# Three shared PSUM banks for projections and transposes in the two attention stages of a hybrid decoder step

## The chip, the cores and the metric

The kernel runs on one NeuronCore of a Trainium2 chip. The metric is the device time of one launch in microseconds (us), taken as the median of the runs shown. All stretches below are in us from the start of the profiled span.

## The reference, cut to what matters

One step of a decoder with two layers runs over 1024 prompt tokens and 8 sample tokens, 1032 columns together. Each layer is a norm, one input projection for all heads, two kinds of heads side by side, an output projection and an MLP:

```python
# layer 0: differential attention (4 heads) and HGRN2 (4 heads)
qa, ka, va, qb, fb, ib, gb = _split(h @ w_in, SPLIT_EVEN)
p = probs(q1, k1) - lam * probs(q2, k2)            # softmax over all earlier keys
return jnp.einsum('bqhk,bkhe->bqhe', ...)          # attention output
# layer 1: forgetting attention (8 heads) and mLSTM (4 heads)
qc, kc, vc, fc, qd, kd, vd, id_, fd, od = _split(h @ w_in, SPLIT_ODD)
s = s + fq - fk                                    # bias from the forget gates
```

The prompt attends to itself. Each of the 8 sample tokens attends to 512 cached tokens, in four pages of 128 that a page table picks from a pool. This second part is called the decode here.

## The kernel before

All activations lie transposed, 128 features on the partitions and 1032 tokens along the columns. A projection makes one block of 128 output features from 8 chunks of the 1024 inputs. It does so for three token blocks of 344 columns, and each of these needs 24 matmuls, since float32 accuracy is had from three passes (`mm3`, L119). The 24 matmuls gather in one PSUM bank, which VectorE then empties into the tile `z` (L183, or L185 with a constant). Below, "block" means such a token block: 24 matmuls and one eviction.

An attention stage is the part of `run` in which the prompt's attention of one layer is computed. Layer 0 has it from about 157 to 517 us and layer 1 from about 1573 to 1987 us. Three strands of work are mixed in it:

- The attention itself (`diff_head`, `fox_head`): scores into the tile `S` (L517, L519, L520), row minimum on VectorE (L535, L537), exponential on ScalarE (L539), transposes of the probabilities into the tile `pm` (L557), the split of these into two parts (`Ph` on ScalarE at L545, `Pl` on VectorE at L546), and the products with the values into the tile `po` (L573). The values are transposed as well (L591, L1067).
- Projections as filler (`self.fill`): 27 blocks for the queries, keys and values of the later heads, then 24 blocks for the layer's other kind of heads. `tick` traces some of them after each score block, and `drain` traces what is left of a list.
- The decode as background (`self.back`, `diff_sample` and `fox_sample`). It begins when the sample queries, which the projections leave in `qa_s` or `qc_s`, are transposed (L659) and written to DRAM (L663). Then each of the 32 key pages is loaded (L653), multiplied on GpSimd (L675) and summed on VectorE (L676). After a softmax each of the 32 value pages is loaded, multiplied (L691) and summed (L692). Four tiles `dk` hold pages. All these loads are issued by SyncE, in order.

The order of the instructions on each engine is not written by hand. A scheduler takes the traced program and places instructions as their operands and a slot of their tile's pool come free; a tile's pool and tag say which slots it may take. In both attention stages PSUM's eight banks are given as follows: four to `S` (two tiles of two banks), one to `po`, two to the tag `m` (all transposes and small products, named `pm` and `hms`) and one to the tag `acc` (the projections).

Of the kernel before, what the change touches and what calls it, by code (L numbers as in the profile page):

```python
# [10 lines left out]
F32 = mybir.dt.float32  # L11
# [7 lines left out]
D = 1024          # model width  # L19
NP = 1024         # prompt tokens  # L20
NS = 8            # sample tokens (one per sequence)
T = NP + NS       # columns of every transposed activation
TB = 344          # token block of a projection
NTB = T // TB
KC = D // 128     # contraction chunks of a projection
NCH = NP // 128   # token chunks of 128
PAGES = 4
# [3 lines left out]
LN_MIN = 1e-19    # smallest argument that Ln is given  # L31
# [5 lines left out]
# columns of the packed per-partition parameters  # L37
# [7 lines left out]
class Tags:  # L45
    """Pools of a phase, stacked in the order in which their tiles are done with (or wanted); tags pick the pool."""
# [9 lines left out]
class Step:  # L56
    """The whole step: two trunk layers over 1032 transposed columns."""

    def __init__(self, tc, ctx, I, O):
# [20 lines left out]
        # scratch in DRAM  # L80
# [11 lines left out]
    def wsplit(self, src, kk, m=128, parts=None):  # L92
        """Loads a block of weights and splits it into two float32r parts."""
        nc = self.nc
        r = self.wr.tile([128, 8, 128], F32, name="wr")
        h, l = parts or (self.wh.tile([128, 8, 128], F32R, name="wh"), self.wl.tile([128, 8, 128], F32R, name="wl"))
        nc.sync.dma_start(r[:, :kk, :m], src)
        nc.scalar.activation(h[:, :kk, :m], r[:, :kk, :m], AF.Copy)  # L98
        nc.gpsimd.tensor_tensor(l[:, :kk, :m], r[:, :kk, :m], raw(h[:, :kk, :m]), op=ALU.subtract)  # L99
        return h, l  # L100

    def first_block(self, src):
        """wsplit of the block that the whole core waits for, in pieces."""
# [9 lines left out]
    def mm3(self, out, h, l, ah, al, ks, sl, m=128):  # L113
        """out = W^T a with float32 accuracy from three float32r passes."""
# [7 lines left out]
    def project(self, ps, src, evict, m=128, w=None):  # L122
        """One block of output features; yields after each token block."""
        h, l = w or self.wsplit(src, KC, m)
        for tb in range(NTB):
            sl = slice(tb * TB, (tb + 1) * TB)
            pt = ps.tile([128, 512], F32, name="acc", tag="acc")
# [4 lines left out]
    def project_rms(self, ps, src, evict, rms, w=None):  # L132
        """The first block of a phase: its products run while 1/rms is still being computed."""
# [9 lines left out]
    def project_to(self, pool, ps, src, dst, scale=None, keep=None, done=None):  # L143
        """A block of output features into DRAM (and its sample columns into keep)."""
# [11 lines left out]
    def tick(self, n=1.0):  # L156
        """Traces the next pieces of the filler work (projections) and of the background work (decode)."""
# [12 lines left out]
    def drain(self, k, upto=None):  # L170
        """Traces what is left of a kind of work (up to and with one generator)."""
# [4 lines left out]
    def scaled(self, dst, scale=None):  # L176
        """Eviction of a projection: times the token's 1/rms (and a constant)."""
# [11 lines left out]
    def gain(self, x, n, gcol, hi, lo):  # L189
        """x * gain of chunk n, split into two float32r parts (the last chunk by token blocks, as it is waited for)."""  # L190
# [16 lines left out]
    def rms(self, pool, ps, sq=None, t0=0, n=T):  # L207
        """rb[:, t] = 1 / sqrt(mean_d x[t, d]^2 + eps) on every partition, for n tokens from t0."""
# [25 lines left out]
    def head_norm(self, sm, po, pm, dst, gcol, gate, n, eps=None, thr=None):  # L234
        """dst = po * rsqrt(mean over partitions of po^2 + eps) * gain (* gate); po stays in PSUM."""
# [17 lines left out]
    def hgrn_gates(self, ph, ps, pr, first):  # L253
        """f = lb + (1 - lb) sigmoid(.) and silu(g) of all heads, into DRAM."""
# [32 lines left out]
        # orders the first Ln behind the last Sigmoid (one table switch)  # L287
# [4 lines left out]
    def ln_exp(self, last):  # L292
        """One table set with both Ln and Exp, loaded behind the layer's last Sigmoid."""
# [3 lines left out]
    def hgrn_unit(self, h, u, ph, ps):  # L297
        """Half of a head's tokens (four chunks), in steps.

        Decays are products of the gates f. With blocks of hh tokens, QP holds q times the product of f from the  # L300
        block's start through the token, KR holds k times the product behind the token to the block's end, and
        pe the products of whole blocks; each level joins pairs of blocks, from 1 token up to a chunk of 128."""
# [17 lines left out]
        # A^T[s, t]: the diagonal, then one level of the binary tree of decays at a time  # L320
# [29 lines left out]
        # rows of the decayed k, states after each chunk  # L350
# [23 lines left out]
        # o^T = i^T A^T + S^T (q e^b), normalised and gated  # L374
# [11 lines left out]
    def staggered(self, units, lag):  # L386
        """Traces units in turn, each some steps behind the one before."""
# [12 lines left out]
    def hgrn_sample(self, ph, ps):  # L400
        """One step of the HGRN2 states: S' = f S + k i, o = q^T S'."""
# [41 lines left out]
    def diff_consts(self, ph, ps):  # L443
        """lambda, the constants made from it, and the Toeplitz tiles of the relative bias."""
# [9 lines left out]
        # c = max(1, |lambda|): probabilities are kept as (p1 - lambda p2) / c  # L454
        nc.vector.tensor_scalar(lc[:, 1:2], lc[:, 0:1], -1.0, 1.0, op0=ALU.mult, op1=ALU.max)
        nc.vector.tensor_tensor(lc[:, 1:2], lc[:, 1:2], lc[:, 0:1], op=ALU.max)
        nc.vector.reciprocal(lc[:, 2:3], lc[:, 1:2])                                    # 1 / c
# [1104 lines left out]
```

## Time and profile before

| quantity | value |
|---|---|
| median of 3 runs | 2928.14 us (2927.41 to 2929.16) |
| span of the profiled execution | 2917.3 us |
| what lies around the span (median less span) | 10.8 us |
| TensorE busy | 2769.9 us, 95% of the span |
| VectorE, ScalarE, GpSimd busy | 1285.9, 891.8 and 871.3 us |
| mean granted clock of TensorE | 0.967 of full speed |

The profile gives no time of its own for the profiled execution besides the span, so the runs' median is set beside it. TensorE is busy nearly all the time in the two MLPs, which fill most of the span. The two attention stages are 774 us together, and it is there that TensorE idles and that its clock falls.

### The profile page before, as it was taken

Reading aid. Unit: us, or ns where it says so; the run is one execution under the profiler, and the core shown is the slowest. Engines: PE = TensorE matmul, PEld = TensorE weight load, DVE = VectorE, ACT = ScalarE, POOL = GpSimd, SP = SyncE. Lnnn points to the kernel's source line nnn. Section 1 sums busy time; section 2 is a strip of 40 time slices with the busy share of each in tenths; the row PEclk is TensorE's granted clock in tenths of the full one; section 3 lists DMA queues with packets and bytes.
Section 4 is the critical chain, followed back from the end, with each engine's and each line's share of the span. In section 5 each row is a group of like instructions: output and inputs, shape, how many; then the busy total and the mean of one; then the engine's idle time right before and its main releaser. Section 6 shows DMA issues by size and latency. Waiting matters only on the chain.

```text
span 2917.3 us, 43680 instructions
## 1 busy us (share of the span) xinstructions
PE 2769.9 (95%) x17276; PEld 2646.3 (91%) x17276; DVE 1285.9 (44%) x2433; ACT 891.8 (31%) x1546; POOL 871.3 (30%) x689
## 2 busy tenths in 40 slices
PE   8999889899999999999999989679999999999997
PEld 7988778898999999999998988577889999999997
DVE  5154866675532233322435455465463333223335
ACT  4143434114321222222323434343342222222223
POOL 2322753354222212222122254331242222221222
PEclk9999999899999999999999999887999999999998
DMA  3343686633111111111224354875331111111111
GB/s 135 117 145 98 200 219 194 167 109 99 48 51 51 48 39 45 52 51 54 74 98 126 115 169 124 164 190 136 105 98 47 37 48 51 51 48 37 48 62 66
DMA packets 167103, 278.48 MB, mean 95 GB/s; under 512 B 25159, under 2 KB 86375, under 8 KB 166899
## 3 DMA queue, kind: packets, MB, share of 16 engines
q1 hardware_dynamic: 166562, 275.42, 31.8%
q8 instruction: 136, 2.23, 0.3%
q0 software_dynamic: 336, 0.28, 0.1%
q14 instruction: 69, 0.56, 0.1%
HBM read 226.53 MB, written 49.11 MB: 94 GB/s over the span
## 4 chain that ended last, share of the span: by engine, by line
PE 79%; DMA 9%; DVE 5%; POOL 2%; issue 2%; ACT 1%; SPq 1%; DVEq 0%; POOLq 0%; ACTq 0%
PE acc L119 69%; DMA dp<-p_c 1%; PE pm L338 1%; PE po L573 1%; PE S L520 1%; PE S L517 1%; DMA kd<-out_ka 1%; PE pm L557 1%; DMA dk<-in_cache_k_c 1%; DMA dI<-irow 1%; POOL dk L691 1%; DMA dk<-in_cache_v_a 1%; POOL dk L675 1%; DMA ol<-os 1%; DMA dk<-in_cache_v_c 1%
## 5 line engine op out<-in xcount | busy, mean ns | idle before, releaser
L119 PE MATMUL acc<-xh,wh 128*128 128x344 f32 (+1 forms) x2808 | 919.2, 328 | 38.6 <-DVE z L183 28.0
L119 PE MATMUL acc<-xl,wh 128*128 128x344 f32 (+1 forms) x2808 | 909.1, 324 | 1.0 <-DVE xl L195 0.9
L99 POOL TENSOR_TENSOR wl<-wr,wh 128x512 fp32r<-128x512 f32 (+1 forms) x284 | 504.5, 1777 | 1350.0 <-ACT wh L98 1347.4
L119 PE MATMUL acc<-xh,wl 128*128 128x344 f32 (+1 forms) x2808 | 902.0, 323 | 3.8 <-POOL wl L99 3.8
L119 PEld LDWEIGHTS acc<-xh,wh 128*128 128x128 f32 (+1 forms) x2808 | 536.3, 191 | 52.2 <-DVE z L183 31.9
L119 PEld LDWEIGHTS acc<-xh,wl 128*128 128x128 f32 (+1 forms) x2808 | 534.8, 191 | 5.6 <-POOL wl L99 4.7
L119 PEld LDWEIGHTS acc<-xl,wh 128*128 128x128 f32 (+1 forms) x2808 | 536.1, 191 | 3.2 <-DVE xl L195 2.3
L98 ACT ACTIVATE wh<-wr 128x512 fp32r<-128x512 f32 (+1 forms) x284 | 228.3, 805 | 974.5 <-PE acc L119 844.2
L119 PE MATMUL acc<-ul,wh 128*128 128x344 f32 (+1 forms) x1568 | 495.6, 317 | 0.2 <-DVE ul L1178 0.2
L119 PE MATMUL acc<-uh,wl 128*128 128x344 f32 (+1 forms) x1568 | 493.9, 317 | 1.5 <-POOL wl L99 1.5
L119 PE MATMUL acc<-uh,wh 128*128 128x344 f32 (+1 forms) x1568 | 493.0, 317 | 1.6 <-ACT wh L98 1.6
L1243 DVE TENSOR_TENSOR x<-acc,x 128x344 f32<-128x344 f32 x336 | 173.5, 516 | 438.1 <-PE acc L119 438.1
L119 PEld LDWEIGHTS acc<-uh,wh 128*128 128x128 f32 x1568 | 294.0, 188 | 2.1 <-ACT wh L98 2.0
L119 PEld LDWEIGHTS acc<-uh,wl 128*128 128x128 f32 x1568 | 293.6, 188 | 2.1 <-POOL wl L99 2.1
L119 PEld LDWEIGHTS acc<-ul,wh 128*128 128x128 f32 x1568 | 294.5, 188 | 0.7 <-DVE ul L1178 0.6
L1230 DVE TENSOR_TENSOR ul<-u,uh 128x344 fp32r<-128x344 f32 x192 | 146.0, 762 | 202.2 <-ACT uh L1229 202.2
L1227 DVE SCALAR_TENSOR_TENSOR t<-acc,rb 128x344 f32<-128x344 f32 x192 | 98.6, 516 | 267.7 <-PE acc L119 265.7
L1228 ACT ACTIVATE u<-t 128x344 f32<-128x344 f32 x192 | 93.8, 490 | 323.5 <-DVE t L1227 322.5
L183 DVE TENSOR_TENSOR z<-acc,rb 128x344 f32<-128x344 f32 x138 | 69.9, 512 | 200.1 <-PE acc L119 183.5
L539 ACT ACTIVATE e<-S,st 128x128 f32<-128x128 f32 (+7 forms) x128 | 94.6, 740 | 145.7 <-DVE st L537 70.2
L691 POOL TENSOR_TENSOR dk<-dk,dp 128x512 f32<-128x512 f32 x64 | 84.3, 1334 | 104.9 <-DMA dk<-in_cache_v_c 43.2
L675 POOL TENSOR_TENSOR dk<-dk,dq 128x512 f32<-128x512 f32 x64 | 84.7, 1347 | 43.3 <-DMA dk<-in_cache_k_c 18.1
(377 smaller groups left out, 3289.8 us busy)
## 6 DMA issues: line engine op xcount, KB each, us to landing
wr<-in_w_up SPq DMA_DIRECT2D x64, 512.0 KB
wr<-in_w_down SPq DMA_DIRECT2D x128, 256.0 KB
wr<-in_w_in_e SPq DMA_DIRECT2D x27, 512.0 KB
wr<-in_w_out SPq DMA_DIRECT2D x48, 256.0 KB
wr<-in_w_in_o SPq DMA_DIRECT2D x24, 512.0 KB
x<-in_x SPq DMA_DIRECT2D x16, 516.0 KB
qd<-qS SPq DMA_DIRECT2D x32, 256.0 KB
dk<-in_cache_k_a SPq DMA_DIRECT2D x32, 256.0 KB
```

The lines of the kernel that those rows point to most:

```text
L98: nc.scalar.activation(h[:, :kk, :m], r[:, :kk, :m], AF.Copy)
L99: nc.gpsimd.tensor_tensor(l[:, :kk, :m], r[:, :kk, :m], raw(h[:, :kk, :m]), op=ALU.subtract)
L119: nc.tensor.matmul(out, lhsT=w[:, k, :m], rhs=a[:, sl], start=(n == 0), stop=(n == last))
L183: nc.vector.tensor_tensor(dst[:, sl], p, rb[:m, sl], op=ALU.mult)
L338: nc.tensor.matmul(pt[:, 64 * c:64 * c + 64].rearrange("p (n t) -> p n t", t=hh), lhsT=k[:, 128 * c:128 * c + 128], rhs=Q[:, n0:n0 + 64 // ...
L539: nc.scalar.activation(e[:, :L], S[:, :L], AF.Exp, bias=st[:, 0:1], scale=-1.0, accum_out=st[:, 1:2])
L675: nc.gpsimd.tensor_tensor(kt[:], kt[:], qb[:], op=ALU.mult)
L691: nc.gpsimd.tensor_tensor(v3, v3, pb[:, :, js], op=ALU.mult)
L1227: nc.vector.scalar_tensor_tensor(t[:], pt[:, :TB], 0.0, self.rb[:, sl], op0=ALU.max, op1=ALU.mult)
L1228: nc.scalar.activation(u[:], t[:], AF.Square)
L1230: nc.vector.tensor_tensor(L[:, sl], u[:], raw(H[:, sl]), op=ALU.subtract)
L1243: nc.vector.tensor_tensor(x[:, sl], pt[:, :TB], self.x[n][:, sl], op=ALU.add)
```

## The change

In both attention stages the projections' own pool (`acc1`, `acc4`) is gone. The pool of the transposes gets three banks under its tag `m`, and the projections take their tiles from that tag. Everywhere else `acc_tag` is `"acc"`, as it was. The tile's name stays `acc`, so that the same rows can be found by name. The layer-1 stage is changed in the same way as layer 0, with `pS4`, `pm4` and `acc4`.

```diff
     def project(self, ps, src, evict, m=128, w=None):
...
-            pt = ps.tile([128, 512], F32, name="acc", tag="acc")
+            pt = ps.tile([128, 512], F32, name="acc", tag=self.acc_tag)
             self.mm3(pt[:m, :TB], h, l, self.xh, self.xl, range(KC), sl, m)
...
         self.credit = {}
+        self.acc_tag = "acc"
...
-            pS, pm, acc = self.pool(st, "pS1", 2, True), self.pool(st, "pm1", 2, True), self.pool(st, "acc1", 1, True)
+            pS, pm = self.pool(st, "pS1", 2, True), self.pool(st, "pm1", 3, True)
+            acc, self.acc_tag = pm, "m"
             hd = self.pools(st, "hd0", "ld dp dk dq row32 sc ov pr tr pse oso dst", "Q1 K1 K2 bias st rl", "z e")
...
             self.drain("fill")
             self.drain("back")
+            self.acc_tag = "acc"
```

The scheduler makes another order of both stages. The first place is TensorE in the attention stage of layer 0, where the transpose of the sample queries stands (`pm` from `qa_s`, L659). The number behind a tile's name rises in the order in which tiles were traced. Before, it stands here, behind the last rows of the block `acc_2220`:

```order
L119 MATMUL acc_2220<-xl7_185,wh_2215 128x344
L119 MATMUL acc_2220<-xh7_184,wl_2216 128x344
L659 MATMUL pm_2537<-ident_72,qa_s_90 32x128
L591 MATMUL pm_2587<-ident_72,vt_2583 128x128 x4
L591 MATMUL pm_2594<-ident_72,vt_2583 128x128 x4
L119 MATMUL acc_2261<-xh0_122,wh_2215 128x344
```

With the change the same transpose, now `pm_2534`, stands here:

```order
L517 MATMUL S_2714<-K1_2428,Q1_2427 128x512
L520 MATMUL S_2714<-K2_2408,Q1_2427 128x512
L240 MATMUL hms_2500<-hsq_2498,ones_73 128x512
L659 MATMUL pm_2534<-ident_72,qa_s_90 32x128
L591 MATMUL pm_2584<-ident_72,vt_2580 128x128 x4
L517 MATMUL S_2807<-K1_2416,Q1_2415 128x512
```

Before, the transpose was taken ahead of blocks that were traced earlier: `acc_2261` comes behind `pm_2537`. With the change every tile of the tag `m` stands in traced order, in both stages, and six more blocks (144 matmuls of L119) stand ahead of the transpose.

The second place is TensorE in the attention stage of layer 1, at the transpose of its sample queries (`pm` from `qc_s`). Before:

```order
L119 MATMUL acc_15690<-xl7_13832,wh_15685 128x344
L119 MATMUL acc_15690<-xh7_13831,wl_15686 128x344
L659 MATMUL pm_15955<-ident_72,qc_s_93 32x128
L557 MATMUL pm_16071<-ident_72,e_15919 128x128
L557 MATMUL pm_16071<-ident_72,e_15999 128x128
```

With the change:

```order
L119 MATMUL acc_15922<-xl7_13828,wh_15917 128x344
L119 MATMUL acc_15922<-xh7_13827,wl_15918 128x344
L659 MATMUL pm_15948<-ident_72,qc_s_93 32x128
L119 MATMUL acc_15995<-xh0_13429,wh_15917 128x344
L119 MATMUL acc_15995<-xl0_13430,wh_15917 128x344
```

Here too the transpose waits for all blocks traced before it (`acc_15922` has a number just below `pm_15948`), which again are 144 more matmuls of L119 than before.

The third place is VectorE at the end of the decode of layer 1, where the last page is summed (the second `ov` row). Before:

```order
L692 TENSOR_REDUCE ov<-dk 128x4
L546 TENSOR_TENSOR Pl<-pm,Ph 128x512
L756 TENSOR_REDUCE oso<-ov 128x32
L183 TENSOR_TENSOR z<-acc,rb 128x344
L757 TENSOR_TENSOR oso<-oso,pse 128x32
L1092 RECIPROCAL st<-st 128x1
L1096 TENSOR_SCALAR e<-e,st 128x896
```

With the change:

```order
L692 TENSOR_REDUCE ov<-dk 128x4 x2
L756 TENSOR_REDUCE oso<-ov 128x32
L183 TENSOR_TENSOR z<-acc,rb 128x344
L757 TENSOR_TENSOR oso<-oso,pse 128x32
L1432 CAST triT<-triTf 128x512
L183 TENSOR_TENSOR z<-acc,rb 128x344
L546 TENSOR_TENSOR Pl<-pm,Ph 128x512 x3
```

Behind the last sum VectorE still had 8 row minima (L535) and 19 splits (L546) of the stage to do before; with the change 4 and 14 are left.

## Rows read from the trace of the kernel before

**Rows 1.** The page: span, and busy time of each engine.

```profile
span 2917.3 us, 43680 instructions
PE 2769.9 (95%) x17276; PEld 2646.3 (91%) x17276; DVE 1285.9 (44%) x2433; ACT 891.8 (31%) x1546; POOL 871.3 (30%) x689
```

**Rows 2.** Windows: stretch, its length, busy time by engine, granted clock, DMA share, GB/s.

```profile
157.00:281.00 124.00, 121.68 (x689) 104.31 (x688) 63.33 (x151) 50.27 (x98) 25.82 (x18) 1.00 0.36 115
281.00:381.00 100.00, 92.30 (x507) 77.92 (x506) 75.02 (x146) 41.49 (x78) 61.50 (x44) 0.95 0.67 192
381.00:478.00 97.00, 85.18 (x425) 71.01 (x425) 68.65 (x141) 37.21 (x70) 57.20 (x38) 0.89 0.85 215
478.00:517.00 39.00, 35.27 (x219) 30.90 (x217) 20.50 (x47) 18.55 (x34) 2.58 (x2) 1.00 0.54 181
1573.00:1690.00 117.00, 107.67 (x697) 102.30 (x696) 52.30 (x96) 47.64 (x87) 27.65 (x18) 0.99 0.39 121
1690.00:1836.00 146.00, 128.88 (x799) 118.25 (x797) 85.40 (x156) 59.63 (x113) 71.02 (x80) 0.93 0.57 148
1836.00:1946.00 110.00, 72.90 (x388) 66.43 (x388) 57.28 (x104) 33.02 (x66) 51.02 (x37) 0.77 0.79 182
1946.00:1987.00 41.00, 36.94 (x231) 32.18 (x231) 24.22 (x49) 26.47 (x52) 2.30 (x9) 0.92 0.45 149
...
506.00:517.00 11.00, 7.33 (x50) 5.87 (x48) 6.48 (x19) 4.71 (x8) 1.28 (x1) 1.00 0.62 210
```

**Rows 3.** TensorE's eviction waits in 157:285, 285:517 (two), 1570:1692, 1692:1987: total, times, longest.

```profile
PE acc L119 <- DVE z L183: 2.0, 3, 0.7
...
PE acc L119 <- DVE z L183: 7.7, 5, 3.8
...
PE acc L119 <- DVE z L185: 1.9, 2, 1.7
...
PE acc L119 <- DVE z L183: 5.2, 8, 0.7
...
PE acc L119 <- DVE z L183: 13.2, 6, 5.1
```

**Rows 4.** The chain that ended last: start, length, what.

```profile
48.83 102.42 PE acc L119 x650
...
264.88 4.07 PE acc L119 x24
...
274.29 4.00 PE acc L119 x24
...
1657.62 4.05 PE acc L119 x24
...
1685.81 4.02 PE acc L119 x24
1690.52 2.55 DMA qrow_c<-row
```

**Rows 5.** Timeline of TensorE near 300 us: the start of two score pairs.

```profile
299.25 0.50 PE L517 MATMUL S<-K,Q 128*128 128x512 f32 x1
...
300.11 0.50 PE L517 MATMUL S<-K,Q 128*128 128x512 f32 x1
```

**Rows 6.** Timeline of GpSimd at the start of layer 0's decode.

```profile
279.00 0.71 POOL L663 DMA_DIRECT2D qrow_a<-row  x1 [1.94 <-ACT row L661]
286.42 8.07 POOL L675 TENSOR_TENSOR dk<-dk,dq 128x512 f32<-128x512 f32 x6 [6.72 <-DMA dq<-qrow_a]
```

**Rows 7.** Waits in 1836:1946 of VectorE, GpSimd, SyncE; last, VectorE in 360:480.

```profile
DVE ov L692 <- POOL dk L691: 50.6, 19, 8.0
...
POOL dk L691 <- DMA dk<-in_cache_v_c: 43.2, 12, 6.2
...
SPq L1165 <- POOL dk L691: 24.0, 10, 3.3
...
DVE ov L692 <- POOL dk L691: 19.6, 12, 3.2
```

More of the change, by code (lines that the diff above doesn't have):

```diff
@@ L1388, in run @@
             self.drain("back")
+            self.acc_tag = "acc"
         with ExitStack() as st:
@@ L1400, in run @@
         with ExitStack() as st:
-            pS, pm, acc = self.pool(st, "pS4", 2, True), self.pool(st, "pm4", 2, True), self.pool(st, "acc4", 1, True)
+            pS, pm = self.pool(st, "pS4", 2, True), self.pool(st, "pm4", 3, True)
+            acc, self.acc_tag = pm, "m"
             hd = self.pools(st, "hd1", "ld dp dk dq row32 sc lg sfx ov pr lfe pse oso dst lgg", "Q1 K1 K2 Q20 Q21 st", "z e")
@@ L1419, in run @@
             self.drain("back")
+            self.acc_tag = "acc"
         with ExitStack() as st:
@@ L1432, in run @@
             self.drain("back")
+            self.acc_tag = "acc"
         with ExitStack() as st:
```

## The prediction

> **What bounds the kernel now.** I began with the page [rows 1]: TensorE is busy 2769.9 of 2917.3 us, so at most 147 us lie idle. The table of windows [rows 2] shows the two attention stages, the only places that the change touches: 774 us, with TensorE busy in 681. Read it by stretch. Each stage opens with a stretch full of TensorE work: 121.7 of 124 us and 107.7 of 117, at a granted clock of 1.00 and 0.99. Then the decode starts [rows 6], and the bound changes. While the value pages pass (381 to 478 and 1836 to 1946), TensorE is busy in 85.2 of 97 us and 72.9 of 110, the clock falls to 0.89 and 0.77, and the DMA engines are the fullest thing, at 0.85 and 0.79. There VectorE waits for GpSimd's products (19.6 us in layer 0, 50.6 in layer 1), GpSimd waits for the pages (43.2), and SyncE waits for GpSimd to free a tile (24.0) [rows 7]. This ring of load, product, sum and next load has only four page tiles; it runs at its own pace, and everything queued behind a sum on VectorE waits with it. Once the decode is over, TensorE leads again for 39 and 41 us.
>
> So a stage is a chain of three parts: work before the decode's start (A), the decode (B), and what is left behind it (tail). A transfer of PSUM matters as far as it changes A, B or the tail.
>
> **What the change removes.** With one bank a block's first matmul waits until VectorE has emptied the block before. These waits sum to 2.0 + 7.7 + 1.9 + 5.2 + 13.2 = 30.0 us in both stages [rows 3]; that is the most they can give. Where blocks follow each other with nothing between, the chain shows the price: six intervals from 1657.62 to 1685.81 are 28.19 us, 4.70 each, while an unbroken run of 650 such matmuls takes 102.42 us, 0.158 each and 3.78 for 24 [rows 4]. Each such block wastes 0.92 us. Layer 1 has eight in a row, 7.4 us in A. In layer 0 the three blocks from 264.88 to the transpose at about 278.1 take 13.3 instead of 11.3 us: 2.0.
>
> The waits inside B (7.7 + 1.9 and 13.2, less what lies in the tail) stand in stretches that the decode paces. I bound their worth by 0 and 22.8 us and take 6, three for each layer, nearer to the lower end, since in 1836 to 1946 TensorE idles 37 us in any case.
>
> **What it moves.** Projections and transposes now take slots of one tag, and the order shows that they take them in traced order. Before, the transposes went ahead: the sample queries' transpose L659 stood ahead of blocks traced earlier. Now it stands behind all of them, 144 matmuls later in each stage: six blocks of 3.78 us, 22.7. Fewer scores stand ahead of it in return: six pairs in layer 0, four in layer 1. A 512-wide pair takes 0.86 us (299.25 to 300.11) [rows 5], so at most 5.2 and 3.4; many are narrower in layer 0, so I take 4.0 and 3.4. Everything that starts the decode hangs on L659: ScalarE's copy, GpSimd's transfer at 279.00, SyncE's query loads, and the first product at 286.42 [rows 6]. On SyncE the page loads, weights and the next heads' keys are queued behind the query loads, so they move too. A grows by
>
> - layer 0: 22.7 - 4.0 - 2.0 = +16.7 us
> - layer 1: 22.7 - 3.4 - 7.4 = +11.9 us
>
> TensorE has as much less to do later. That pays only where TensorE leads. In B of layer 0 four fewer evictions stand on VectorE among the decode's sums. If TensorE led there, 15 us would come back; if the decode leads, nothing. With the DMA at 0.85 of 16 engines and TensorE busy in 88% of the value pages' stretch, I take 4 us, about a quarter. In layer 1, B has six blocks fewer, but six scores and five splits more, moved in from the tail: nothing comes back.
>
> **The tail.** In layer 0 it is one block shorter and one score longer: nothing. In layer 1 the order leaves 4 row minima instead of 8 and 14 splits instead of 19. The tail is 41 us [rows 2]; three blocks of it (11.3 us) stay. Of the other 29.7 I count per split, since splits fill it: 5 of 19 is 7.8 us, by minima half, 14.9. I take 11.
>
> **The sum.** Layer 0: 16.7 - 4 - 3 = +9.7. Layer 1: 11.9 - 3 - 11 = -2.1. Together +7.6 us on the span of 2917.3. I add 3 us for new stalls: stretches of over 40 attention matmuls with no projection between stand twice in the order before and ten times with the change, and one of the old ones, at 506 to 517, has TensorE busy in only 7.3 of 11 us [rows 2]. Each could thus cost up to 3.7 us, 30 for the eight new ones; most of them fall in B, where TensorE waits anyway, so I take a tenth. The span becomes 2928, and with the 10.8 us that the runs' median has around the profiled span, 2938.7 us.
>
> **A rule against this forecast.** In 1573 to 1690, where the eight wasted gaps stand, the granted clock is 0.99 [rows 2], which is the upper of the two levels; it falls only where the decode makes TensorE wait for long. The Trainium skill, page "TensorE: Matmul & The Clock Gate", section "A second HAM failure mode: psum-queue depth-cycling", says that short idle times of TensorE between groups of matmuls, made by cycling through PSUM banks, make the clock oscillate. By that rule taking the gaps away would give clock back as well; this trace does not agree, as the gaps stand at 0.99 (what the rule would give is in rival 1). [...]
>
> **Rivals.**
>
> 1. *TensorE leads in B too, and the eviction waits are simply gone.* For it: TensorE is busy in 92 of 100 us from 281 to 381, and 129 of 146 from 1690 to 1836 [rows 2]. Then the later start costs nothing, since the blocks done early are missing later, and 30.0 us come back: 2928.1 - 30 = 2898. If the tail of layer 1 shrinks on top, 2887. Against it: from 1836 on TensorE idles 37 us of 110. It decides from the point at which the decode, started 12 to 17 us later, still ends no later. With clock regained besides, in proportion: the four stretches of B lie 5%, 11%, 7% and 23% below full clock, which is 51 us of their 453 lost; eviction waits are 22.8 of their 74 us of idle time, so 16 us of it, 2882. Of the chance of 0.24, this has 0.04. The psum-queue rule above would make it so.
> 2. *A draw.* The value pages run faster since fewer evictions sit between their sums, and the 15 us of layer 0 come back in full: 2938.7 - 11 = 2928. For it: VectorE is the second fullest engine from 281 to 381, 75 of 100 us [rows 2]. Chance 0.20.
> 3. *The clumps cost the whole price.* With projections used up early, the eight new stretches without filler each cost 3.7 us: 2938.7 - 3 + 30 = 2966. For it: VectorE and ScalarE need a row minimum, an exponential, a scaling and two splits for every few matmuls. Against it: in the tail of layer 1, 41 us almost without filler, TensorE is still busy in 36.9. Chance 0.17.
> 4. *The forecast*: the decode starts 12 to 17 us later and layer 0 ends later by most of that, layer 1 gives it back in its tail: 2939. Chance 0.39.
>
> **How the numbers follow.** A difference of 0.2% (5.9 us) is about what a measurement of this kernel can tell from none. Faster takes rival 1 and a little of the draw: 0.26. Same takes most of the draw and the lower edge of the forecast: 0.23. Slower takes the rest of the forecast and rival 3: 0.51. The range leaves out the farther half of rivals 1 and 3: 2903 to 2964. The forecast's own range is 2930 to 2950.
>
> **What would show it.** In the changed profile, `qrow_a` should be sent about 15 us later than 279.0, and `qrow_c` 10 to 14 us later than 1690.5. The evictions' waits on TensorE should nearly vanish. The value pages' stretches should keep about 95 and 110 us. Layer 0's stage should end near 527, and layer 1's tail be some 11 us shorter. The forecast is wrong if the decode catches up, which would show as key pages passing faster than before, or if TensorE waits for `Pl` in the long attention stretches by more than 10 us in all.

## The result, and the profile after

The changed kernel takes 3004.32 us (median, 2999.97 to 3010.24), the kernel before in the same comparison 2928.65 (2927.41 to 2930.74): a ratio of 1.0252, with a 95% interval of 1.0233 to 1.0270. It is 75.7 us slower. The forecast had the sign (2938.7), but the result lies above its range (2903 to 2964).

The profiled execution of the changed kernel took 3002.92 us, 1.8 more than its span, and all later profiles have these 1.8 us around them too. The span of 2917.3 [rows 1] thus belongs to an execution that was about 9 us faster than the median, so the two spans overstate the change: they differ by 83.8 us, the medians by 75.7. The page of the changed kernel:

```profile
span 3001.1 us, 43700 instructions
PE 2803.1 (93%) x17276; PEld 2666.2 (89%) x17276; DVE 1276.1 (43%) x2433; ACT 893.6 (30%) x1546; POOL 866.5 (29%) x689
```

TensorE has as many instructions as in [rows 1], but is busy 33.2 us longer with them. The mean granted clock went from 0.967 to 0.949; whether all of the 33.2 us is the clock is not shown. The other 51 us are idle time of TensorE.

To see where, cut layer 0's stage at the same events in both traces: the sample queries leave, the softmax of the sample rows reaches TensorE, the first and the last sum of a value page, the end of the stage. Windows of the kernel before (columns as in [rows 2]):

```profile
158.00:279.00 121.00, 118.68 (x672) 101.94 (x672) 61.76 (x148) 48.85 (x96) 25.11 (x17) 1.00 0.36 113
279.00:362.00 83.00, 75.30 (x416) 65.08 (x414) 66.37 (x125) 34.06 (x64) 57.75 (x40) 0.94 0.67 192
362.00:382.00 20.00, 20.00 (x112) 15.52 (x110) 10.12 (x25) 8.47 (x17) 5.46 (x6) 1.00 0.63 192
382.00:476.00 94.00, 82.18 (x415) 69.19 (x414) 66.46 (x133) 36.21 (x67) 55.72 (x37) 0.89 0.86 218
476.00:520.00 44.00, 37.27 (x227) 32.05 (x225) 25.17 (x73) 19.55 (x34) 3.06 (x3) 0.97 0.55 178
```

And of the changed kernel, below them layer 1's stage, which answers to the lower half of [rows 2] (its second and third row together to 1690 to 1836 there, 158 us where it was 146):

```profile
160.00:304.00 144.00, 141.62 (x814) 126.61 (x812) 59.03 (x143) 48.71 (x91) 31.01 (x21) 0.97 0.34 107
304.00:406.00 102.00, 83.73 (x414) 69.58 (x413) 65.33 (x134) 37.68 (x71) 55.57 (x38) 0.83 0.61 166
406.00:429.00 23.00, 21.89 (x92) 16.31 (x92) 12.89 (x34) 9.82 (x19) 2.95 (x5) 0.78 0.26 78
429.00:526.00 97.00, 68.76 (x293) 51.76 (x291) 57.98 (x117) 31.86 (x59) 52.42 (x36) 0.73 0.77 202
526.00:585.00 59.00, 49.16 (x260) 40.66 (x259) 27.62 (x78) 20.43 (x36) 2.56 (x2) 0.85 0.41 132
...
1642.00:1774.00 132.00, 127.45 (x822) 123.17 (x821) 52.69 (x96) 48.58 (x83) 32.98 (x22) 0.97 0.39 122
1774.00:1900.00 126.00, 104.25 (x618) 93.49 (x618) 79.41 (x148) 52.82 (x105) 61.70 (x71) 0.86 0.45 125
1900.00:1932.00 32.00, 23.68 (x160) 21.41 (x159) 13.79 (x29) 15.09 (x31) 9.64 (x8) 0.95 1.01 177
1932.00:2038.00 106.00, 65.91 (x330) 57.27 (x331) 54.67 (x102) 31.12 (x61) 46.12 (x34) 0.73 0.77 175
2038.00:2070.00 32.00, 28.22 (x180) 25.02 (x180) 17.40 (x34) 19.43 (x36) 1.77 (x8) 0.95 0.54 178
```

Read the two by row. Ahead of the decode TensorE now does 142 matmuls more, and that stretch is 23 us longer. What those matmuls were taken from is the rest: 293 instead of 415 during the value pages. But the rest is no shorter. From the queries' start to the softmax TensorE does about as many matmuls (414, before 416; 240 of them projections, before 264) in 102 us instead of 83, at a clock of 0.83 instead of 0.94. The value pages take 97 instead of 94 us, as rigid as they were thought to be. The tail is 15 us longer, with 260 matmuls instead of 227 and a clock of 0.85 instead of 0.97. From the decode's start to the end of the stage TensorE does 1059 matmuls instead of 1170, is busy longer with them (223.5 us against 214.8), and idles 57 instead of 26 us.

The waits of projections for their own eviction [rows 3] are gone. Other waits stand in their place. TensorE's longest in 303:429, in 429:530 and, for layer 1, in 1774:2070 (line, what it waited for: total, times, longest):

```profile
PE pm L557 <- DVE e L622: 9.4, 2, 7.8
PE pm L557 <- DVE hrs L245: 3.9, 1, 3.9
...
PE S L517 <- ACT e L539: 6.9, 4, 5.3
PE S L517 <- DVE Q L506: 6.8, 1, 6.8
PE po L573 <- ACT Ph L545: 5.7, 3, 4.8
PE pm L557 <- DVE e L622: 3.3, 1, 3.3
...
PE pm L557 <- DVE z L183: 27.0, 6, 6.7
PE S L517 <- ACT e L539: 15.5, 9, 6.4
PE po L573 <- DVE Pl L546: 11.3, 11, 3.5
```

In layer 0 these are transposes that wait for scaled rows (`e`), scores that wait for an exponential to free their bank or for a new head's `Q`, and value products that wait for a split: links of the attention chain with no projection to put beside them. In layer 1 the largest is new: a transpose waits until VectorE has emptied a projection's block (`z`), since they share the slots. It takes 27.0 us, where the projections' own waits took 5.2 + 13.2 us [rows 3]. The wait for `Pl` is not new. In the kernel before it was the largest of layer 1, and it fell from 21.5 to 11.3 us (the kernel before, 1692:1987):

```profile
PE po L573 <- DVE Pl L546: 21.5, 5, 13.4
```

### The profile page after: what moved, and what is told of

It reads as the page before. It is cut to its first block, busy times and chain, and to the rows that moved or that the text cites. A ratio compares the mean times of both kernels' runs of the same rounds, so it can differ in the third digit from the quotient of the medians.

```text
span 3001.1 us, 43700 instructions
## 1 busy us (share of the span) xinstructions
PE 2803.1 (93%) x17276; PEld 2666.2 (89%) x17276; DVE 1276.1 (43%) x2433; ACT 893.6 (30%) x1546; POOL 866.5 (29%) x689
## 4 chain that ended last, share of the span: by engine, by line
PE 78%; DMA 10%; DVE 5%; POOL 2%; ACT 2%; issue 1%; SPq 1%; DVEq 0%; POOLq 0%; ACTq 0%
PE acc L119 68%; DMA dk<-in_cache_v_c 2%; PE po L573 2%; PE S L520 1%; PE S L517 1%; PE pm L338 1%; DMA dk<-in_cache_k_c 1%; DMA dp<-p_c 1%; DMA kd<-out_ka 1%; PE pm L557 1%; DMA dI<-irow 1%; DMA dk<-in_cache_v_a 1%; DVE xl L195 1%; DVE sq L205 1%; POOL dk L691 1%
## 5 line engine op out<-in xcount | busy, mean ns | idle before, releaser
L119 PE MATMUL acc<-xh,wh 128*128 128x344 f32 (+1 forms) x2808 | 914.2, 326 | 10.4 <-ACT xh L194 8.0
L119 PE MATMUL acc<-xl,wh 128*128 128x344 f32 (+1 forms) x2808 | 907.8, 324 | 0.6 <-DVE xl L195 0.5
L119 PE MATMUL acc<-xh,wl 128*128 128x344 f32 (+1 forms) x2808 | 900.2, 322 | 3.9 <-POOL wl L99 3.9
L119 PEld LDWEIGHTS acc<-xh,wh 128*128 128x128 f32 (+1 forms) x2808 | 535.3, 191 | 17.9 <-ACT xh L194 8.0
L119 PEld LDWEIGHTS acc<-xl,wh 128*128 128x128 f32 (+1 forms) x2808 | 534.6, 190 | 4.7 <-issue 2.5
L119 PEld LDWEIGHTS acc<-xh,wl 128*128 128x128 f32 (+1 forms) x2808 | 533.7, 190 | 5.1 <-POOL wl L99 4.7
L119 PE MATMUL acc<-ul,wh 128*128 128x344 f32 (+1 forms) x1568 | 495.6, 317 | 0.5 <-DVE ul L1178 0.5
L119 PE MATMUL acc<-uh,wl 128*128 128x344 f32 (+1 forms) x1568 | 493.8, 317 | 1.5 <-POOL wl L99 1.5
L119 PE MATMUL acc<-uh,wh 128*128 128x344 f32 (+1 forms) x1568 | 493.1, 317 | 2.1 <-ACT wh L98 2.1
L119 PEld LDWEIGHTS acc<-uh,wh 128*128 128x128 f32 x1568 | 294.0, 188 | 2.6 <-ACT wh L98 2.5
L119 PEld LDWEIGHTS acc<-ul,wh 128*128 128x128 f32 x1568 | 294.5, 188 | 1.0 <-DVE ul L1178 0.9
L119 PEld LDWEIGHTS acc<-uh,wl 128*128 128x128 f32 x1568 | 293.7, 188 | 1.9 <-POOL wl L99 1.9
L557 PE MATMUL pm<-ident,e 128*128 128x128 f32 x432 | 77.3, 309 | 59.8 <-DVE z L183 30.1
L517 PE MATMUL S<-K,Q 128*128 128x512 f32 (+2 forms) x192 | 86.8, 455 | 36.3 <-ACT e L539 23.5
```

The costliest lines, as they stand in the source:

```text
L119: nc.tensor.matmul(out, lhsT=w[:, k, :m], rhs=a[:, sl], start=(n == 0), stop=(n == last))
L517: nc.tensor.matmul(S[:, cs], lhsT=Q1[:, qs], rhs=K1[:, cs], start=True, stop=False)
L557: nc.tensor.transpose(pt[:, n:n + 128], P[r][:, 128 * kb:128 * kb + 128], self.ident[:])
```

## The experiments

Three theories stood against each other. **D** is the step on which the prediction rested: the decode starts later, and that carries through. **F** is about the order as a whole: since one tag hands out its slots in traced order, a transpose can no longer go ahead of projections traced before it; the projections come early and in clumps, later stretches of attention have nothing beside them, TensorE idles there and its clock falls; and the decode's softmax, which stands behind 41 tiles of scores on TensorE in both kernels, is reached late. **S**: sharing the banks costs something by itself.

In the edited kernels the line numbers are shifted; the tiles' names are the same.

The built orders say what is meant. Number the projection blocks of layer 0's stage. Ahead of the transposed tiles, one after the other, the kernel before has issued 4, 4, 5, 7, 7, 10, 10, 11, 11, 12, 12, 14, 14, 16 blocks, and 22 ahead of L659; the changed kernel 2, 2, 2, 8, 8, 8, 16, 16, 16, 27, 27, 27, 27, 27 and 27.

**One layer at a time.** Layer 1 gets its own banks back (`l0_only`); the other kernel does the same to layer 0.

```diff
-            pS, pm = self.pool(st, "pS4", 2, True), self.pool(st, "pm4", 3, True)
-            acc, self.acc_tag = pm, "m"
+            pS, pm, acc = self.pool(st, "pS4", 2, True), self.pool(st, "pm4", 2, True), self.pool(st, "acc4", 1, True)
```

> Only layer 0's attention stage shares its banks; layer 1's stands as before. The two profiles so far put layer 0 at +65 to +69 us (from the start of its attention to the first block of its MLP) and layer 1 at +15. If the two stages are independent: 2928 + 67 = 2995 us, within 10. If part of the loss comes from one stage disturbing the other: under 2980 or over 3005. Theory F (the shared tag puts projections and transposes in traced order, the filler is used up early, and TensorE idles and loses clock in long stretches of attention) and theory D (the decode starts later and everything behind it moves) both allow this value; the run sizes the part.

> Only layer 1's attention stage shares its banks. If the stages are independent: 2928 + 15 = 2943 us, within 8. Theory F: long attention stretches without filler (64, 42, 42 and 72 matmuls in the order) cost some 3 to 4 us each, 12 to 16 in all. Theory D: the decode of layer 1 starts 12 to 15 us later and its tail gives 8 to 11 back, so 2930 to 2936.

Measured: 2979.59 us, ratio 1.0189 (1.0163 to 1.0215), and 2934.31 us, 1.0037 (1.0023 to 1.0052), against 2921.94 on that chip. Layer 0 alone costs 57.7 us and layer 1 alone 12.4, together 70.1 of the 75.7: within the intervals the two add up, and layer 0 has four fifths. As differences both lie in what was expected of independent stages, 57.7 at its lower edge. Layer 1's 12.4 lies in F's 12 to 16 and beyond D's 2 to 8, but by its ratio it is 10.8 us, between the two. (The ratios are those on record for each comparison; they differ from the quotients of the medians by up to 0.2%, so numbers in us and ratios agree only to some 6 us.)

**The queries early.** In the changed kernel the transpose of the sample queries is traced right behind the projection that makes them.

```diff
+    def query_rows(self, ph, ps, src, name):
...
+        self.qrow = self.rows_to_dram(ph, ps, src, name)
+        return
+        yield
...
+            qkv.insert(7, self.query_rows(hd, pm, self.qa_s[:], "qrow_a"))
```

> Both stages share their banks, but the transpose of the sample queries is traced right behind the projection that makes them, so it stands behind 24 acc matmuls fewer than in the kernel before in each layer, instead of 120 to 144 more. Theory D (the late start of the decode is the cause): the decode starts as early as before, and most of the 76 us comes back, 2930 to 2955 us. Theory F (filler used up early): the order still has stretches of 67, 60, 54 and 44 attention matmuls without filler in layer 0; only what hangs on the start of the decode comes back, 25 us at most, 2980 to 3005 us.

Measured: 2997.62 us, 1.0244 (1.0213 to 1.0274). It gains nothing, which lies in F's range. GpSimd's timeline shows that the queries leave 6.4 us earlier than in [rows 6], and 31.6 us earlier than in the changed kernel, whose row stands second:

```profile
272.62 0.71 POOL L663 DMA_DIRECT2D qrow_a<-row  x1
...
304.25 0.71 POOL L663 DMA_DIRECT2D qrow_a<-row  x1 [8.57 <-ACT row L661]
```

The key pages pass from 286.1 to 359.5 us, as early as in the kernel before (287.7 to 357.3). Yet the first value sum comes at 430.5, as late as in the changed kernel (429.0). The sums of the key and of the value pages (duration, first and last start):

```profile
L682 DVE TENSOR_REDUCE sc<-dk x32: 660/683/690, 286.1 to 359.5; 128x8 f32<-128x512 f32 x32
...
L698 DVE TENSOR_REDUCE ov<-dk x32: 669/687/692, 430.5 to 519.4; 128x4 f32<-128x512 f32 x32
```

What lies between is the softmax of the sample rows, which begins on TensorE. Its row (duration, first and last start) in the kernel before:

```profile
L713 PE MATMUL S<-ohd,tr x2: 587/612/638, 362.2 to 362.6; 32*64 32x512 f32 x2
```

In the changed kernel:

```profile
L713 PE MATMUL S<-ohd,tr x2: 587/612/638, 406.2 to 406.7; 32*64 32x512 f32 x2
```

With the queries early:

```profile
L719 PE MATMUL S<-ohd,tr x2: 587/613/639, 410.7 to 411.2; 32*64 32x512 f32 x2
```

The last key sum is 51 us old by then. (It is 5 us old in the kernel before, and 16 in the changed kernel, where it comes at 390.3.) In the order on TensorE 41 score tiles stand ahead of this matmul, and they come slowly. The window of this kernel from the queries' start to shortly before the softmax:

```profile
272.00:406.00 134.00, 119.40 (x545) 96.56 (x544) 84.72 (x177) 50.42 (x98) 59.99 (x43) 0.79 0.50 145
```

So in layer 0 of the changed kernel the decode's start is not all that holds the value pages back. D as the explanation of the whole falls.

**The queries late.** The reverse, in the kernel before with its own banks: L659 alone is issued behind the last block traced ahead of it, so that 1458 matmuls of projections stand ahead of it, as in the changed kernel (1338 before). All other transposes may still go ahead.

```diff
+        self.last_mm = mm.ins
...
-        nc.tensor.transpose(pt[:32, :128], src, self.ident[:])
+        if name in ("qrow_a", "qrow_c"):
+            with self.tc.issue_after(self.last_mm):
+                nc.tensor.transpose(pt[:32, :128], src, self.ident[:])
```

> The kernel before with its own banks, with one thing changed: the transpose of the sample queries in both attention stages is issued behind the last projection block traced ahead of it, so that it stands behind 1458 and 8510 matmuls of projections, the same counts as in the changed kernel (1338 and 8366 in the kernel before). All other transposes may go ahead of projections as before. Theory D (the decode's later start is what carries through): by the prediction's own terms 18.7 us more ahead of the decode in layer 0 and 15.3 in layer 1, of which at least 15 us and at most all 34 reach the end, a ratio of 1.005 to 1.012, and the sample queries leave near 299 us instead of 279. Theory F (what counts is how evenly the projections are spread over the attention's work, and where the decode's softmax stands): the attention keeps its filler apart from six blocks that are taken ahead of this one transpose, so the queries leave as late as theory D says but the whole stays within 0.4 per cent of the kernel before, and no stretch of layer 0's decode has a granted clock under 0.85.

Measured: 2961.45 us against 2934.07, 1.0092 (1.0076 to 1.0107): 27.4 us. That is within D's range for the time and beyond F's, and the value pages ran at a clock of 0.82, which F had excluded. The queries leave later than D said, at 306.2 instead of near 299. The windows of its layer 0:

```profile
158.00:306.00 148.00, 142.04 (x808) 123.31 (x808) 65.26 (x157) 51.71 (x99) 30.10 (x21) 1.00 0.34 106
306.00:388.00 82.00, 76.03 (x402) 64.20 (x401) 62.07 (x121) 34.85 (x65) 56.27 (x39) 0.92 0.70 197
388.00:415.00 27.00, 27.00 (x150) 21.45 (x148) 16.11 (x39) 13.84 (x26) 5.14 (x5) 1.00 0.54 138
415.00:511.00 96.00, 80.71 (x373) 66.60 (x374) 58.56 (x127) 31.26 (x60) 51.81 (x37) 0.82 0.75 206
511.00:543.00 32.00, 21.41 (x107) 17.81 (x106) 20.78 (x61) 15.44 (x29) 1.27 (x1) 0.82 0.62 204
```

Against the kernel before, the start is 27 us later, the stretch with the key pages (82 us, before 83) and the value pages (96, before 94) keep their length, the stretch between the two is 7 us longer (27, before 20), and the tail gives 12 us back (32, before 44). The stage ends 23 us later. This is the prediction's chain of A, rigid B and tail, with its layer-0 term of 9.7 us measured at 23. D holds as a cause; by itself it costs a third as much as the change. It is not a wholly clean test: the five blocks that now stand ahead of L659 are missing later, and the built order ends layer 0's attention with 78 matmuls without a projection, where the kernel before has about 50 (506:517 in [rows 2]).

**The order without the shared banks.** Own banks as before, but each tile's first TensorE instruction is issued behind that of the tile traced before it.

```diff
+    def linked(self, first):
...
+        if self.link is None:
+            r = first()
+        else:
+            with self.tc.issue_after(self.link):
+                r = first()
+        self.link = r.ins
+        return r
...
-        nc.tensor.transpose(pt[:32, :128], src, self.ident[:])
+        self.linked(lambda: nc.tensor.transpose(pt[:32, :128], src, self.ident[:]))
```

> The kernel before, with its own bank for the projections and two for the transposes, but each tile's first TensorE instruction is queued behind that of the tile traced before it, in both attention stages: the traced order alone, without the shared banks. Theory F in its form that the traced order is the cause: 2985 to 3030 us (with one bank the eviction waits, up to 0.9 us per block in a row, come on top). In its form that running ahead through three slots is the cause: 2930 to 2955 us, since one bank lets no block run ahead. Theory D: the transpose that starts the decode stands behind 120 matmuls more, as in the changed kernel, so 2950 to 2975 us.

Measured: 3054.13 us, 1.0443 (1.0425 to 1.0461). The traced order, with one bank for the projections, costs 132 us, more than F's highest 3030 us; D's 2950 to 2975 falls. Its waits on TensorE in layer 0's stage:

```profile
PE acc L131 <- DVE z L196: 18.3, 19, 5.8
PE S L530 <- ACT K L510: 13.4, 4, 5.1
PE po L587 <- DVE Pl L559: 12.0, 7, 6.7
PE S L530 <- ACT e L552: 11.0, 7, 4.8
```

The eviction waits are back (18.3 us) and the attention's own waits come on top. In traced order the kernel with three shared banks is thus 1.0443 - 1.0252 = 1.9%, 56 us, faster than the one with separate banks. That is the distance of two kernels, not a term of the loss.

**The order of before with the shared banks.** A table now says how many blocks are traced ahead of each transposed tile. `same_order` has the counts that the kernel before issued; `plan_after`, the control, those of the changed kernel; `plan_a` those of before up to the decode's start and of the changed kernel behind it; `plan_b` the other way round. Banks are shared in all four.

```diff
+    def planned(self):
+        """Ahead of each transposed tile: as many blocks as the plan has ahead of it."""
+        if self.plan is not None and self.plan:
+            self.ensure(self.plan.pop(0))
...
-            self.fill, self.back = (3.2, qkv), (0, [])
+            self.fill, self.back = (0, []), (0, [])
+            self.work = qkv + [self.hgrn_project(hd, acc, j) for g in range(4) for j in (12 + g, 20 + g)]
```

> Three shared banks as in the change, but the projections are traced by a table: ahead of each transposed tile stand as many blocks as the kernel before issued ahead of it, so that the traced order of the shared tag is the order that the kernel before ran in. Theory F (the order that the shared tag forces is the whole loss): as fast as the kernel before or faster by a part of its 30 us of eviction waits, 0.990 to 1.003 of it. Rival S (sharing itself costs, because a block and a transpose wait for each other's banks): still slower, 1.010 or more.

> Control of the table: the same code as in the run with the order of before, with the block counts that the changed kernel has in its traced order. If the table does what it says, this is the changed kernel again: 1.020 to 1.030 of the kernel before by either theory. Another value means that the table itself (another place of the stores and of the last blocks) moves the time.

> The table has the counts of the kernel before up to the transpose that starts the decode, and those of the changed kernel behind it. Theory F in the form that the filler used up early in the first stretch is the loss: 1.000 to 1.006 of the kernel before. In the form that the clumps behind the decode's start are the loss (the order has attention stretches of 54, 52 and 48 matmuls in layer 0 and 71, 55 and 58 in layer 1): 1.010 to 1.020. Rival S: 1.010 or more.

> The other half: counts of the changed kernel up to the transpose that starts the decode, those of the kernel before behind it, as far as they are not overtaken already. The filler is used up early, and the order has one stretch of 146 attention matmuls without filler in layer 0 and one of 131 in layer 1. Theory F, early use: 1.012 to 1.028. Theory F, late clumps: 1.003 to 1.012. Rival S: 1.010 or more.

| kernel | median us | ratio | interval | queries leave | softmax | first, last value sum |
|---|---|---|---|---|---|---|
| before (events of its first profile) | 2933.62 | 1 | | 279.0 | 362.2 | 381.8, 475.2 |
| `same_order` | 2951.60 | 1.0067 | 1.0042 to 1.0091 | 279.5 | 391.1 | 411.9, 510.3 |
| `plan_b` | 2972.98 | 1.0155 | 1.0115 to 1.0195 | 300.9 | 395.3 | 421.1, 520.1 |
| `plan_a` | 2983.36 | 1.0178 | 1.0150 to 1.0206 | 280.7 | 389.0 | 409.4, 505.4 |
| `plan_after` | 2999.03 | 1.0230 | 1.0201 to 1.0259 | 303.1 | 405.3 | 430.3, 523.3 |

The control gives the loss again, so the table as such is a fair stand-in. With the order of before the same shared banks lose 0.7% instead of 2.3%: 47 of the 65 us that the control lost are the order. The 0.7% lies between what F (at most 1.003) and S (at least 1.010) had expected, so neither is the whole. Both halves of the order matter, and neither form of F that names one half alone holds. With only the part behind the decode's start as in the changed kernel (`plan_a`), the queries leave on time and the ratio is still 1.1% above `same_order`; with only the part ahead of it (`plan_b`) it is 0.9% above. The late queries are in the second and not in the first, for which D has no name. Nor has the late softmax of layer 0: it stands in `plan_a` where it stands in `same_order` (389.0 and 391.1). By the two profiles `plan_a` loses 8 us in layer 0's stage (395.3 to 403.1 us, from the first score to the first matmul of `pm` from `hq`) and 26 in layer 1's (403.1 to 428.9, from the first score to the last `ft`). There TensorE's longest wait is again that of transposes for a projection's eviction (`plan_a`, 1600:2050):

```profile
PE pm L575 <- DVE z L199: 35.4, 7, 12.9
```

**What is left at the order of before.** The same table with the banks of before.

```diff
-            pS, pm = self.pool(st, "pS1", 2, True), self.pool(st, "pm1", 3, True)
-            acc, self.acc_tag = pm, "m"
+            pS, pm, acc = self.pool(st, "pS1", 2, True), self.pool(st, "pm1", 2, True), self.pool(st, "acc1", 1, True)
```

> The table with the order of before, but the banks of before too: one for the projections, two for the transposes. It splits the 0.67% that was left with the same order in three shared banks (ratio 1.0067). If sharing itself costs (rival S, for that rest): 0.997 to 1.003 of the kernel before. If the rest comes from tracing by the table (blocks traced later have another priority against scores and products): 1.004 to 1.010.

Measured: 2935.57 us against 2931.10, 1.0019 (1.0008 to 1.0030), with the softmax at 361.9 and the value pages from 382.0 to 479.3, nearly as before. So of the 0.67% of `same_order` 0.2% comes with the table and about 0.5% (14 us) with sharing, as S expected for the rest. By the profiles it is a sum of two signs: against `own_planned` the stage of layer 0 is 25 us longer (370.4 to 395.3) and that of layer 1 is 9 us shorter (411.8 to 403.1). The windows of `same_order` show where layer 0 loses:

```profile
281.00:357.00 76.00, 60.82 (x259) 48.41 (x258) 55.79 (x110) 28.06 (x49) 52.53 (x38) 0.79 0.66 192
357.00:391.00 34.00, 33.64 (x199) 29.92 (x198) 17.96 (x46) 13.50 (x30) 5.13 (x3) 0.98 0.26 85
```

The same 76 us in the kernel before:

```profile
281.00:357.00 76.00, 68.30 (x372) 58.48 (x371) 60.30 (x110) 31.35 (x59) 57.04 (x39) 0.93 0.72 205
```

The key pages take equally long, but TensorE gets 259 matmuls done beside them instead of 372, at 0.79 instead of 0.93. The rest has to be done behind them, with no page passing, and the softmax comes 29 us later. In shared slots a transpose that waits for VectorE holds a slot that a projection could have, and the other way round (the 27.0 us above). The first shows in layer 1 of `same_order`, where projections wait for the split of a transposed tile (1600:2050):

```profile
PE acc L119 <- DVE Pl L563: 10.2, 2, 6.4
```

That this makes the 25 us of layer 0 was argued, not taken apart by a run.

**Filler later.** If early filler costs, later filler might gain: the table less two blocks everywhere, with 21 blocks ensured ahead of the queries' transpose, with own and with shared banks. The row is shown against that of `same_order`, and cut.

```diff
-            self.plan, self.blocks = [4, 4, 5, 7, 7, 10, 10, 11, 11, 12, 12, 14, 14, 16, 22, ...
+            self.plan, self.blocks = [2, 2, 3, 5, 5, 8, 8, 9, 9, 10, 10, 12, 12, 14, 20, ...
```

> The same lag of two blocks with the banks of before. Theory F: blocks are traced behind the attention and fill its waits by what comes free, 0.990 to 1.000 of the kernel before. If the order of before was as good as any: 0.998 to 1.006.

> Three shared banks, and the table lags by two blocks: ahead of each transposed tile two blocks fewer are traced than the kernel before issued. Theory F (filler ahead of the attention is the loss): better than the order of before in shared banks, 0.997 to 1.005 of the kernel before, since attention goes first and blocks are left for its waits. If a shift of two blocks is nothing against the rest: 1.004 to 1.010 as with the order of before. Rival S: 1.005 or more.

Measured: 2976.39 us, 1.0163 (1.0146 to 1.0180), and 2976.38, 1.0156 (1.0142 to 1.0170). I expected no loss or a gain, and that fell: two blocks later cost 45 us. With shared banks this lies in S's range, but own banks lose as much, so at this order sharing adds nothing. The queries leave on time (278.6 with own banks), but the value pages take 116 us (394.4 to 510.7) instead of 93. With own banks, the longest waits of TensorE in that stage, and below them VectorE's longest in 394:511:

```profile
PE acc L119 <- DVE z L201: 14.8, 4, 6.3
PE pm L575 <- DVE e L642: 8.5, 2, 4.3
...
DVE ov L713 <- POOL dk L712: 48.6, 18, 6.4
```

VectorE waits 48.6 us for the decode's products while the value pages pass, where it waited 19.6 before [rows 7], and evictions stand behind those sums. Why a shift of two blocks costs that much I did not settle. No version beat the kernel before.

## Why the prediction was wrong

**Right.** The sign, though in part by luck: the late start that was to give it costs 27 us by itself, but undone in the changed kernel it wins nothing back. That the projections no longer wait for their evictions (in layer 1 the transposes do instead); that L659 stands later and the queries leave later (304.25 against 279.00); that the value pages keep their length (97 and 105 us from first to last sum, before 93 and 108); that layer 1's tail shrinks (41.4 to 32.4 us, 9.0 where 11 was taken).

**Wrong, by terms of the sum.** Measured between the same events in the two profiles. Terms of some 7 us are within what two executions differ by: in `l1_only` layer 0's stage is the unchanged one, and its profile has it 7 us longer than that of the kernel before (369.1 against 362.1).

| term | predicted | measured |
|---|---|---|
| layer 0: A | +16.7 | +22.8 (120.9 to 143.7) |
| layer 0: decode to last value sum | -7 | +25.3 (196.2 to 221.5) |
| layer 0: tail | 0 | +14.3 (45.0 to 59.3) |
| layer 1: A | +11.9 | about +15 (117 to 132) |
| layer 1: decode to last value sum | -3 | +7.7 (254.7 to 262.4) |
| layer 1: tail | -11 | -9.0 |
| new stalls | +3 | not apart from the above |

The terms sum to 76 us, where 10.6 was predicted; the other 8 us of the 83.8 lie outside the two stages. The step that failed is "so I take a tenth". Eight new long stretches without a projection were counted, each priced at up to 3.7 us from one old stretch, and nine tenths struck off because "most of them fall in B, where TensorE waits anyway". Two things are wrong with that. First, the waits are not hidden in B. From the decode's start to the end of layer 0's stage TensorE idles 31 us more than before. The second half of B, the value pages, starts with the softmax on TensorE, which stands behind 41 score tiles. The softmax comes 44 us later (362.2 to 406.2): 25 us are the late queries, 8 are the key pages, which start 1 us later behind the queries and take 7 longer, and 11 are the wait for TensorE to get there after the last key sum (16 us instead of 5). Second, the price was counted in idle time alone. Where TensorE idles more, the granted clock is lower as well: 0.83 with 18 of 102 us idle, before 0.94 with 8 of 83, and 0.73 with 28 of 97, before 0.89 with 12 of 94; in 406 to 429, behind such a stretch, it is still 0.78 with 1 us idle. The matmuls then took longer, 0.202 us of busy time each in the first of these pairs, before 0.181. Over the four windows from the decode's start to the end of layer 0's stage, length times missing clock is 102 x 0.17 + 23 x 0.22 + 97 x 0.27 + 59 x 0.15 = 57 us, before 83 x 0.06 + 94 x 0.11 + 44 x 0.03 = 17 us. Idle time and lost clock overlap, so the two can't simply be added; how the loss divides between them stays open, and so does why layer 0's tail is longer.

In A of layer 0 a count was wrong as well. Ahead of L659 stand 1458 instead of 1338 matmuls of projections, five blocks and not six (in layer 1 it is six); with 18.9 us for them the term is +12.9, and the miss is 9.9. Two things go into it. In the changed kernel 31 of the projections' matmuls that stood ahead of the first score stand behind it, 4.9 us at 0.158 each. And the clock is low at the start of A, where few blocks have been issued. The changed kernel's two stages, then layer 1 of the kernel before:

```profile
160.00:200.00 40.00, 38.32 (x208) 34.07 (x207) 14.81 (x43) 12.45 (x27) 7.50 (x5) 0.91 0.43 135
200.00:304.00 104.00, 103.30 (x608) 92.54 (x606) 44.21 (x100) 36.26 (x64) 23.51 (x16) 1.00 0.30 96
1642.00:1680.00 38.00, 33.64 (x203) 31.43 (x202) 20.04 (x37) 15.35 (x29) 10.14 (x6) 0.91 0.56 172
1680.00:1774.00 94.00, 93.81 (x621) 91.74 (x620) 32.65 (x59) 33.22 (x54) 22.83 (x16) 1.00 0.32 102
...
1573.00:1611.00 38.00, 33.22 (x214) 31.15 (x213) 25.60 (x46) 20.16 (x39) 9.91 (x6) 0.96 0.57 173
1611.00:1690.00 79.00, 74.44 (x485) 71.15 (x484) 26.70 (x52) 27.48 (x49) 17.74 (x12) 1.00 0.30 96
```

By the missing clock that is an estimated 3.6 us in layer 0 (40 x 0.09), and in layer 1 3.4 where it was 1.5 before (38 x 0.09, 38 x 0.04). In layer 1 the 7.4 us for the gaps is also more than the 5.2 us that TensorE waited there [rows 3].

The DMA engines were called the fullest thing while the value pages pass. In layer 0 they are not: they stand at 0.85, and TensorE is busy in 0.88 of that stretch [rows 2].

**The chain from a late decode** was right as a mechanism (`late_q`), and its size was off: in layer 0 the start is 27 us later where 18.7 stood without the gaps, the softmax adds 7, and the tail gives 12 back where TensorE was to win 4. In the changed kernel neither these 4 us nor the 3 of the evictions showed. But the chain is not what the changed kernel ends by: made early again (`early_q`), the decode is held by the softmax instead, and nothing is won. In layer 0 two causes, each enough to make the value pages late, hide each other: taking one away shows nothing, while adding it alone shows 27 us.

**The rivals.** Rival 3, the clumps at their whole price, was the nearest. It was 38 us short; the clock and the softmax, which it did not price, are the likely rest, but were not sized apart. The sign named against the forecast, TensorE waiting for `Pl` by more than 10 us, says nothing: it showed in layer 1 with 11.3 us, but the kernel before already had 21.5. The larger new waits, for `z` and `e`, had not been named. Rival 1 fell: behind the decode's start layer 0 has 111 matmuls fewer, but TensorE is busy with them 9 us longer. By the rule of the Trainium skill, page "TensorE: Matmul & The Clock Gate", section "A second HAM failure mode: psum-queue depth-cycling", taking away the short gaps between groups should have given clock back. The traces here do not agree: where the gaps stood (1611 to 1690) the clock was 1.00 with them, and in 1680 to 1774, where no projection waits for an eviction any more, it is 1.00 as well, so there was nothing to give back.

## What to carry to other kernels

A PSUM tag is also a queue: here tiles that share one took its slots in traced order, so look at what may overtake what before merging two. In this kernel background matmuls were worth most where the foreground waits; spent early they went with more idle time and a lower clock for what was left, and traced two blocks later everywhere they lost too. When a late event has two causes, test each alone in the kernel before as well as undone in the kernel after.

## What the runs showed of the hardware

A stretch with about as many matmuls (414 and 416, with 240 and 264 of projections) took 102 or 83 us, with the granted clock at 0.83 or 0.94. Gaps of 0.92 us behind blocks of 24 matmuls cost no clock: it was 1.00 with them (1611 to 1690) and without them (1680 to 1774). The mean busy time of a matmul from the decode's start to the end of that stage rose from 0.184 us (214.8 by 1170) to 0.211 (223.5 by 1059); the mixture differs (578 of the 1059 are of projections, before 698 of 1170), so not all of it need be the clock. I had not expected that TensorE can have fewer matmuls and be busy for longer.
